# Gate weights folded between the row scales and the first evacuations, in an fp32-split encoder block

## The chip, the cores and the metric

One of the eight cores of a Trainium2 chip runs the kernel. The metric is device microseconds of one execution, the median over several runs. PE is TensorE (matmuls), DVE is VectorE, ACT is ScalarE, POOL is GpSimd, SP is the engine that issues most DMAs. Each takes its instructions strictly in the order in which they stand in its own queue and waits on semaphores for the others.

## The reference

One encoder layer on x of 512 positions by 1024 channels, float32. Only the first part matters here: RMS norm, one big input projection, a depthwise conv with SiLU on the 2048 mLSTM channels, block-diagonal q, k, v, and input and forget gates that are linear in q, k, v.

```python
h = rmsnorm(x, norm_w[l])                       # x * rsqrt(mean(x*x) + 1e-6) * norm_w
proj = h @ w_in[l]
x_f, z_f, x_m, z_m, o_m, g_logits = jnp.split(proj, split_points, axis=-1)
...
x_c = jax.nn.silu(centred_dwconv(x_m, conv_w[l], conv_b[l]))
q = block_diag_proj(x_c, w_q[l])                # blocks of 4 x 4
k = block_diag_proj(x_c, w_k[l])
v = block_diag_proj(x_m, w_v[l])
qkv = jnp.concatenate([q, k, v], axis=-1)
i_fwd = transpose(qkv @ w_igate_fwd[l] + b_igate_fwd[l])
f_fwd = log_sigmoid(transpose(qkv @ w_fgate_fwd[l] + b_fgate_fwd[l]))   # and both for bwd
...                                             # mLSTM in chunks both ways, Fourier branch, merge, norm
```

## The kernel before

Every large product is made of three matmuls. A float32 operand is split into a high part that TensorE's fp32r format holds (`hi_of`, an ACT copy) and the rest (`lo_of`, a DVE subtraction), and `mm3` adds high*high, high*low and low*high (lines 97 to 99). x is split once, scaled by norm_w, into the tiles hhi and hlo. Everything is laid out with channels in partitions, so one *unit* is 128 output channels of a projection: a weight tile of 128x1024 (8 blocks of 128 input channels), 24 matmuls of 128x512 into one PSUM bank `acc`. The raw weights of a unit come by DMA into a ring of three `raw` tiles (`fetch`, on SP), are split into `whi` and `wlo` (`prepare`), of which there are two buffers each, and are used by `proj`. `unit` prepares one unit ahead, so a unit's high half can be written only when PE has finished the unit two before it.

The row scales of the RMS norm are not applied to x but to the products. ACT squares the eight x tiles (L249), DVE adds them (L252), `norm_rows` sums over channels by matmuls with a column of ones (L311), DVE makes mean plus epsilon from that (rc, L312), POOL raises it to -0.5 (L313). `norm_bcast` puts the four scale columns on diagonals (L318, ACT), multiplies them with ones on PE (L320) and copies the result to SBUF as `rb` (L321, ACT): the 512 scales in every partition. `evac` multiplies a finished bank with rb (L366, DVE).

Units run in this order. Units 0 to 2 (one z unit and the first two conv units) are interleaved while x arrives (`first_units`). Units 3 to 16 are the other conv units, two more z units follow. Unit 3 carries the broadcast as a hook: `RB_AT = (3, 2)` puts it before its third block. From unit 3 on each bank is evacuated, from unit 4 on (`CONV_AT`) each evacuated tile goes through `conv`: one ACT operation, four DVE multiply-adds (L333), a Silu on ACT (L335).

The gate weights are folded with the blocks of q, k, v, so that the gates are products of the conv output and of its input. `load_gates` loads six tiles of 128x512 into the places of x tiles (vhi0, vlo0, vhi1, vlo1, vhi2, vlo2), which are free after the splits and the squares; `fold_gates(n)` multiplies one by the block weights and sums over four (two DVE operations, L282 and L283). In the kernel before the loads are issued with unit 5 and one fold goes with each of units 8 to 13; the last of them also fills `w_gate` (tiles wf0, wf1; L287 DVE, L288 ACT). `gate_mm` then makes the 32 gate matmuls (L301), after the second to last unit of this part; the first of them reads the output of the last conv.

What sets the order: a scheduler in the framework estimates durations and reorders instructions of each engine, except that those wrapped in `pin` keep their program order among one another. The code's order is therefore not always the queue's order.

Of the kernel before, what the change touches and what calls it, by code (L numbers as in the profile page):

```python
# [26 lines left out]
RB_AT = (3, 2)  # L27
LOAD_AT, FOLD_AT, CONV_AT, DRAIN_AT = 5, 8, 4, 12
# [12 lines left out]
def hybrid_block(ctx: ExitStack, tc, xT, xn, first, units, blocks, vecs, gates, gbias, consts, dft, fnw, out):  # L41
# [100 lines left out]
    def prepare():  # L142
        i = state["split"]
        r = raw_unit(i)
        extra = i >= first_pair and i % 4 >= 2
        hi = tl("gwh" if extra else "whi", [P, 1024], F32R, bufs=2)
        lo = tl("gwl" if extra else "wlo", [P, 1024], F32R, bufs=2)
        w = 1024 if len(plan[i]) == 2 else plan[i][0].shape[1]
        hi_of(hi[:, 0:w], r[:, 0:w])
        lo_of(lo[:, 0:w], r[:, 0:w], hi[:, 0:w])  # L150
        items.append((hi, lo))
        state["split"] += 1
        fetch()
# [91 lines left out]
    for g in range(2):  # L245
        part = []
        for k in range(4):
            sq = tl(f"{('sa', 'sb')[g]}{k}", [P, S])
            pin(se.activation(sq, xt[4 * g + k], AF.Square))  # L249
            part.append(sq)  # L250
        for k in range(1, 4):
            ve.tensor_tensor(out=part[0], in0=part[0], in1=part[k], op=ALU.add)  # L252
        sqs.append(part[0])

# [9 lines left out]
    grep, folded = {}, []  # L264
# [10 lines left out]
    def fold_gates(n):  # L275
        if n == 0:
            folds.extend([tl("vhi3", [P, 2, 16, 16]), tl("vlo3", [P, 1, 16, 16])])
        j, half = n // 2, n % 2
        hs = slice(8 * half, 8 * half + 8)
        g = grep[j, half]  # L280
        w = wview((V_WQ, V_WK, V_WV)[j])[:, hs].unsqueeze(2).to_broadcast([P, 8, 16, 4])
        pin(ve.tensor_tensor(out=g, in0=g, in1=w, op=ALU.mult))  # L282
        ve.tensor_reduce(out=folds[j // 2][:, j % 2, hs, :], in_=g, axis=AX.X, op=ALU.add)  # L283
        if n == 5:
            folded.append(True)
            f = folds[0]
            ve.tensor_tensor(out=w_gate[0][:, :, 0:16], in0=f[:, 0], in1=f[:, 1], op=ALU.add)  # L287
            se.activation(w_gate[1][:, :, 0:16], folds[1][:, 0], AF.Copy)  # L288
# [18 lines left out]
    def norm_rows():  # L307
        ssq = bank("wk", cols=4)
        for b in range(4):
            for g in range(2):  # L310
                pin(te.matmul(ssq[:, b : b + 1], sqs[g][:, b * P : (b + 1) * P], ones[:, 0:1], start=g == 0, stop=g == 1))  # L311
        ve.tensor_scalar(out=rc, in0=ssq, scalar1=1.0 / D, scalar2=EPS, op0=ALU.mult, op1=ALU.add)  # L312
        gp.tensor_tensor(out=rc, in0=rc, in1=mhalf[:, 0:1].to_broadcast([P, 4]), op=ALU.pow)  # L313

    def norm_bcast():
        diag = tl("sa15", [P, 4, P])
        for b in range(4):
            se.activation(diag[:, b], ident, AF.Copy, scale=rc[:, b : b + 1])  # L318
        rbp = bank("wk")
        pin(te.matmul(rbp, ones, diag.rearrange("p b c -> p (b c)"), start=True, stop=True))  # L320
        se.activation(rb, rbp, AF.Copy)  # L321
# [21 lines left out]
    def first_units():  # L343
        accs = [bank(t) for t in ("acc", "wk", "acc")]
        for n in range(4):
            for i, ((wh, wl), acc) in enumerate(zip(firsts, accs)):
                last = n == 3 and i == 2
                if last:
                    norm_rows()
# [5 lines left out]
    def proj(hooks={}):  # L355
        wh, wl = unit()
        acc = bank("acc")
        for k in range(8):
# [3 lines left out]
            mm3(acc, wh[:, ks], wl[:, ks], hv(x_hi, k), hv(x_lo, k), k == 0, k == 7, any(at <= k for at in hooks))  # L362
        return acc

    def evac(dst, acc, func=None):
        ve.tensor_tensor(out=dst, in0=acc, in1=rb, op=ALU.mult)  # L366
# [16 lines left out]
    for n, (kind, i) in enumerate([("z", 0)] + [("x", i) for i in XO]):  # L383
# [3 lines left out]
        acc = early[n] if n < NU0 else proj(hooks)  # L387
# [6 lines left out]
        if n >= RB_AT[0]:  # L394
            for j, *args in waiting:
                evac(*args)
# [3 lines left out]
        if n == LOAD_AT:  # L400
            load_gates()
        if n >= CONV_AT and ready:
            conv(ready.pop(0))
        while n >= DRAIN_AT and ready:
            conv(ready.pop(0))
        if FOLD_AT <= n < FOLD_AT + 6:
            fold_gates(n - FOLD_AT)
# [741 lines left out]
```

## Time and profile before

| | |
|---|---|
| median of three runs | 766.57 us (764.42 to 767.64) |
| the profiled execution | 765.64 us, its span 763.5 us |
| mean granted TensorE clock | 0.995 |
| PE busy | 751.3 us, 98% of the span |
| DVE, ACT, POOL busy | 526.3, 412.6, 69.0 us |
| DMA | 128.55 MB, mean 168 GB/s |

The span runs from the first to the last instruction of the core; the time of the execution is about 2 us longer. In rows of the profile the first number is a start in us from the beginning of the span, the second a duration; `[0.52 <-ACT whi L90]` means that the engine sat idle 0.52 us before and that ACT's write of whi at line 90 ended it. In a table of stretches each engine has its busy time and, in brackets, the number of its instructions; PEclk is the granted clock. L-numbers are lines of the kernel before. Matmuls overlap, so a stretch with PE busy throughout is judged by how far apart the matmuls start.

### The profile page before, as it was taken

Reading aid. Unit: us, or ns where it says so; the run is one execution under the profiler, and the core shown is the slowest. Engines: PE = TensorE matmul, PEld = TensorE weight load, DVE = VectorE, ACT = ScalarE, POOL = GpSimd, SP = SyncE. Lnnn points to the kernel's source line nnn. Section 1 sums busy time; section 2 is a strip of 40 time slices with the busy share of each in tenths; the row PEclk is TensorE's granted clock in tenths of the full one; section 3 lists DMA queues with packets and bytes.
Section 4 is the critical chain, followed back from the end, with each engine's and each line's share of the span. In section 5 each row is a group of like instructions: output and inputs, shape, how many; then the busy total and the mean of one; then the engine's idle time right before and its main releaser. Section 6 shows DMA issues by size and latency. Waiting matters only on the chain.

```text
span 763.5 us, 10954 instructions
## 1 busy us (share of the span) xinstructions
PE 751.3 (98%) x4146; PEld 645.2 (85%) x4146; DVE 526.3 (69%) x820; ACT 412.6 (54%) x649; POOL 69.0 (9%) x147
## 2 busy tenths in 40 slices
PE   9999999999999999999999999999999999999996
PEld 8778884888888888888888888899999999988885
DVE  7499993687758565866585757257667687556876
ACT  7444456559456842785264343266544577543444
POOL 0000000013200400041002110000020100000003
PEclk9999999999999999999999999999999999999998
DMA  8157766175852883378404973367655446554452
GB/s 299 55 206 234 225 191 197 50 216 154 175 174 85 253 203 122 120 211 224 135 28 150 224 236 117 101 197 210 193 165 152 135 153 197 176 180 144 145 193 110
DMA packets 40805, 128.55 MB, mean 168 GB/s; under 512 B 4785, under 2 KB 5426, under 8 KB 35634
## 3 DMA queue, kind: packets, MB, share of 16 engines
q1 hardware_dynamic: 36658, 104.14, 40.5%
q0 software_dynamic: 3520, 23.07, 15.0%
q8 instruction: 32, 0.52, 0.3%
q10 hardware_dynamic: 576, 0.66, 0.2%
q14 instruction: 19, 0.16, 0.1%
HBM read 125.76 MB, written 44.04 MB: 222 GB/s over the span
## 4 chain that ended last, share of the span: by engine, by line
PE 95%; DVE 2%; ACT 1%; issue 1%; POOL 0%; POOLq 0%; ACTq 0%
PE acc L97 17%; PE acc L99 17%; PE acc L98 17%; PE wk L97 7%; PE wk L99 7%; PE wk L98 7%; PE acc L556 3%; PE acc L557 3%; PE acc L558 3%; PE wk L627 2%; PE acc L999 1%; PE acc L998 1%; PE acc L997 1%; PE wk L301 1%; PE wk L659 1%; PE wk L196 1%
## 5 line engine op out<-in xcount | busy, mean ns | idle before, releaser
L93 DVE TENSOR_TENSOR wlo<-raw,whi 128x1024 fp32r<-128x1024 f32 (+2 forms) x107 | 125.1, 1172 | 79.5 <-ACT whi L90 78.3
L90 ACT ACTIVATE whi<-raw 128x1024 fp32r<-128x1024 f32 (+2 forms) x107 | 108.6, 1019 | 121.8 <-PE acc L98 71.1
L97 PE MATMUL acc<-hhi,whi 128*128 128x512 f32 x240 | 95.2, 397 | 0.7 <-ACT whi L90 0.7
L99 PE MATMUL acc<-hhi,wlo 128*128 128x512 f32 x240 | 94.0, 393 | 1.2 <-DVE wlo L93 1.2
L98 PE MATMUL acc<-hlo,whi 128*128 128x512 f32 x240 | 94.0, 392 | 0.0
L93 DVE TENSOR_TENSOR gwl<-raw,gwh 128x1024 fp32r<-128x1024 f32 (+1 forms) x39 | 47.2, 1209 | 18.0 <-ACT gwh L90 17.9
L90 ACT ACTIVATE gwh<-raw 128x1024 fp32r<-128x1024 f32 (+1 forms) x39 | 40.9, 1049 | 31.6 <-PE acc L98 11.2
L97 PEld LDWEIGHTS acc<-hhi,whi 128*128 128x128 f32 x240 | 45.5, 190 | 11.7 <-ACT whi L90 1.6
L99 PEld LDWEIGHTS acc<-hhi,wlo 128*128 128x128 f32 x240 | 45.4, 189 | 11.3 <-DVE wlo L93 1.7
L98 PEld LDWEIGHTS acc<-hlo,whi 128*128 128x128 f32 x240 | 45.4, 189 | 9.5 <-issue 0.2
L558 PE MATMUL acc<-whi,hlo 128*128 128x512 f32 x128 | 50.4, 394 | 0.0
L557 PE MATMUL acc<-wlo,hhi 128*128 128x512 f32 x128 | 50.4, 393 | 0.0
L98 PE MATMUL acc<-sb,whi 128*128 128x512 f32 x128 | 50.1, 391 | 0.0
L97 PE MATMUL acc<-sa,whi 128*128 128x512 f32 x128 | 49.8, 389 | 0.0
L98 PE MATMUL wk<-vlo,phi 128*128 128x512 f32 x128 | 49.8, 389 | 0.0
L97 PE MATMUL wk<-vhi,phi 128*128 128x512 f32 x128 | 49.6, 389 | 0.0
L99 PE MATMUL acc<-sa,wlo 128*128 128x512 f32 x128 | 49.0, 391 | 0.0
L99 PE MATMUL wk<-vhi,plo 128*128 128x512 f32 x128 | 48.0, 389 | 0.0
L556 PE MATMUL acc<-whi,hhi 128*128 128x512 f32 x128 | 47.7, 393 | 0.0
L333 DVE SCALAR_TENSOR_TENSOR t2k<-sa,vecs,t2k 128x511 f32<-128x511 f32 (+1 forms) x64 | 45.4, 744 | 0.3 <-ACT t2k L330 0.3
L93 DVE TENSOR_TENSOR vlo<-wk,vhi 128x512 fp32r<-128x512 f32 x32 | 20.6, 677 | 16.3 <-ACT vhi L90 16.3
L98 PEld LDWEIGHTS wk<-vlo,phi 128*128 128x128 f32 x128 | 24.0, 188 | 5.0
(411 smaller groups left out, 1916.8 us busy)
## 6 DMA issues: line engine op xcount, KB each, us to landing
raw<-in_units_dram SPq DMA_DIRECT2D x69, 512.0 KB, 4.1
sum<-in_blocks_dram SPq DMA_DIRECT2D x20, 1024.0 KB, 8.3
raw<-sum SPq DMA_DIRECT2D x64, 256.0 KB, 3.6
raw<-in_blocks_dram SPq DMA_DIRECT2D x48, 256.0 KB, 3.9
sum<-in_blocks_dram POOLq DMA_DIRECT2D x10, 1024.0 KB, 9.8
sum<-sum POOLq DMA_DIRECT2D x10, 1024.0 KB, 8.8
raw<-sum SPq DMA_DIRECT2D x8, 512.0 KB, 4.4
raw<-in_blocks_dram SPq DMA_DIRECT2D x6, 512.0 KB, 4.2
```

The costliest lines, as they stand in the source:

```text
L90: pin(se.activation(dst, src, AF.Copy, scale=scale), pinned)
L93: pin(ve.tensor_tensor(out=dst, in0=src, in1=hi.bitcast(F32), op=ALU.subtract), pinned)
L97: pin(te.matmul(acc, wh, xh, start=start, stop=False, **skip), pinned)
L98: te.matmul(acc, wh, xl, start=False, stop=False, **skip)
L99: te.matmul(acc, wl, xh, start=False, stop=stop, **skip)
L196: te.matmul(junk[:, 0:P], ones, ones, start=True, stop=True)
L301: pin(te.matmul(gate_ps[rows, :], w_gate[j][:, i, :], r, start=n == 0, stop=n == 14, tile_position=(0, 32 * (2 * b + j))), n + b + j > 0)
L333: ve.scalar_tensor_tensor(out=cv[:, o], in0=src[:, s], scalar=cw[k], in1=cv[:, o], op0=ALU.mult, op1=ALU.add)
L556: te.matmul(ops[t], hv(x_hi, k)[:, ts], wh[:, ks], start=k == 0, stop=False)
L557: te.matmul(ops[t], hv(x_hi, k)[:, ts], wl[:, ks], start=False, stop=False)
L558: te.matmul(ops[t], hv(x_lo, k)[:, ts], wh[:, ks], start=False, stop=k == 7)
L627: te.matmul(vp[:, ds], xm[c0 + d][:, b * P : (b + 1) * P], vbf[:, d, :], start=True, stop=True)
```

## The change

Nothing of the arithmetic's meaning changes; one addition replaces another. Its parts:

- The two sums of squares are added on DVE, so that `norm_rows` needs four matmuls instead of eight.
- `load_gates` is called in `first_units`, before the row sums, and the six folds stand right behind the row scales (before unit 3's matmuls in the program). `fill_gates` is a function of its own, called at unit 12.
- Units 3 and 4 are prepared before the row sums; the splits of the units up to 5 counted from the first prepared (i <= NU0 + 2) are pinned, and so are rc, the diagonals, rb, the folds, the evacuations of the banks that have waited, and the matmuls of unit 4.
- The broadcast stands before the fifth block of unit 3 (`RB_AT = (3, 4)`), and the first evacuations come with unit 4 instead of unit 3.

```diff
-RB_AT = (3, 2)
-LOAD_AT, FOLD_AT, CONV_AT, DRAIN_AT = 5, 8, 4, 12
+RB_AT = (3, 4)
+CONV_AT, DRAIN_AT = 4, 12
...
-        hi_of(hi[:, 0:w], r[:, 0:w])
-        lo_of(lo[:, 0:w], r[:, 0:w], hi[:, 0:w])
+        hi_of(hi[:, 0:w], r[:, 0:w], pinned=i <= NU0 + 2)
+        lo_of(lo[:, 0:w], r[:, 0:w], hi[:, 0:w], pinned=i <= NU0 + 2)
...
+    ve.tensor_tensor(out=sqs[0], in0=sqs[0], in1=sqs[1], op=ALU.add)
...
-        ve.tensor_reduce(out=folds[j // 2][:, j % 2, hs, :], in_=g, axis=AX.X, op=ALU.add)
-        if n == 5:
-            folded.append(True)
-            f = folds[0]
-            ve.tensor_tensor(out=w_gate[0][:, :, 0:16], in0=f[:, 0], in1=f[:, 1], op=ALU.add)
-            se.activation(w_gate[1][:, :, 0:16], folds[1][:, 0], AF.Copy)
+        pin(ve.tensor_reduce(out=folds[j // 2][:, j % 2, hs, :], in_=g, axis=AX.X, op=ALU.add))
+
+    def fill_gates():
+        f = folds[0]
+        ve.tensor_tensor(out=w_gate[0][:, :, 0:16], in0=f[:, 0], in1=f[:, 1], op=ALU.add)
+        pin(se.activation(w_gate[1][:, :, 0:16], folds[1][:, 0], AF.Copy))
...
-            for g in range(2):
-                pin(te.matmul(ssq[:, b : b + 1], sqs[g][:, b * P : (b + 1) * P], ones[:, 0:1], start=g == 0, stop=g == 1))
-        ve.tensor_scalar(out=rc, in0=ssq, scalar1=1.0 / D, scalar2=EPS, op0=ALU.mult, op1=ALU.add)
+            pin(te.matmul(ssq[:, b : b + 1], sqs[0][:, b * P : (b + 1) * P], ones[:, 0:1], start=True, stop=True))
+        pin(ve.tensor_scalar(out=rc, in0=ssq, scalar1=1.0 / D, scalar2=EPS, op0=ALU.mult, op1=ALU.add))
...
                 if last:
+                    load_gates()
+                    prepare()
+                    prepare()
                     norm_rows()
...
+        if n == NU0:
+            for m in range(6):
+                fold_gates(m)
-        acc = early[n] if n < NU0 else proj(hooks)
+        acc = early[n] if n < NU0 else proj(hooks, n == NU0 + 1)
...
-        if n >= RB_AT[0]:
+        if n > RB_AT[0]:
             for j, *args in waiting:
-                evac(*args)
+                evac(*args, pinned=len(waiting) > 1 and j != i)
...
-        if n == LOAD_AT:
-            load_gates()
...
+        if n == DRAIN_AT:
+            fill_gates()
...
-        if FOLD_AT <= n < FOLD_AT + 6:
-            fold_gates(n - FOLD_AT)
```

How the queues move at three places. In their rows stand line, operation, the tile written, `<-` and the tiles read, and a size; numbers tell buffers and writes of a name apart. The lines of the changed kernel lie one to four lines higher (L283 for L282, L369 for L366).

DVE before, from rc to the low half of unit 5 (wlo_70); sz0, sa4, sa5 are the evacuations of units 0 to 2, sa6 and sa7 of 3 and 4, t2k tiles are convs:

```order
L312 TENSOR_SCALAR rc_50_240<-wk_54_310 128x4
L366 TENSOR_TENSOR sz0_55_327<-acc_51_241,rb_49_239 128x512
L366 TENSOR_TENSOR sa4_57_329<-wk_52_242,rb_49_239 128x512
L366 TENSOR_TENSOR sa5_58_330<-acc_53_243,rb_49_239 128x512
L333 SCALAR_TENSOR_TENSOR t2k_74_415<-sa4_57_329,vecs_11_108,t2k_74_415 128x510
L333 SCALAR_TENSOR_TENSOR t2k_87_468<-sa5_58_330,vecs_11_108,t2k_87_468 128x510
L333 SCALAR_TENSOR_TENSOR t2k_74_415<-sa4_57_329,vecs_11_108,t2k_74_415 128x511
L366 TENSOR_TENSOR sa6_68_376<-acc_65_343,rb_49_239 128x512
L366 TENSOR_TENSOR sa7_73_413<-acc_72_388,rb_49_239 128x512
L333 SCALAR_TENSOR_TENSOR t2k_87_468<-sa5_58_330,vecs_11_108,t2k_87_468 128x511
L93 TENSOR_TENSOR wlo_70_383<-raw_61_335,whi_69_382 128x1024
```

DVE in the change, the same place; four pairs of L283 and L284 on vhi0, vlo0, vhi1 and vlo1 stand between rc and the first row here, and wlo_78 is unit 5's low half:

```order
L283 TENSOR_TENSOR vhi2_58_319<-vhi2_58_319,vecs_11_108 128x512
L288 TENSOR_TENSOR wf0_44_230<-vhi3_71_352 128x16x16
L284 TENSOR_REDUCE vlo3_72_353<-vhi2_58_319 128x128
L283 TENSOR_TENSOR vlo2_59_321<-vlo2_59_321,vecs_11_108 128x512
L284 TENSOR_REDUCE vlo3_72_353<-vlo2_59_321 128x128
L93 TENSOR_TENSOR wlo_78_401<-raw_62_327,whi_77_400 128x1024
L369 TENSOR_TENSOR sz0_67_348<-acc_51_242,rb_49_240 128x512
L369 TENSOR_TENSOR sa4_69_350<-wk_52_243,rb_49_240 128x512
L369 TENSOR_TENSOR sa5_70_351<-acc_53_244,rb_49_240 128x512
L369 TENSOR_TENSOR sa6_76_399<-acc_73_366,rb_49_240 128x512
L369 TENSOR_TENSOR sa7_81_431<-acc_80_406,rb_49_240 128x512
L333 SCALAR_TENSOR_TENSOR t2k_82_438<-sa4_69_350,vecs_11_108,t2k_82_438 128x510
```

The folds and the fill of wf0 now lie between rc and unit 5's low half, and that low half lies ahead of all evacuations instead of behind five of them and four conv steps.

PE before, from the end of unit 3 (acc_65) to unit 5 (acc_79) and unit 6 (acc_92); unit 4 is acc_72:

```order
L97 MATMUL acc_65_343<-hhi3_18_133,whi_59_331 128x512
L98 MATMUL acc_65_343<-hlo3_22_137,whi_59_331 128x512
L99 MATMUL acc_65_343<-hhi3_18_133,wlo_60_332 128x512
L98 MATMUL acc_72_388<-hlo3_22_137,whi_62_337 128x512
L99 MATMUL acc_72_388<-hhi3_18_133,wlo_63_338 128x512
L97 MATMUL acc_79_429<-hhi0_15_130,whi_69_382 128x512
L98 MATMUL acc_79_429<-hlo0_19_134,whi_69_382 128x512
L97 MATMUL acc_92_482<-hhi0_15_130,whi_76_423 128x512
L98 MATMUL acc_92_482<-hlo0_19_134,whi_76_423 128x512
L99 MATMUL acc_79_429<-hhi0_15_130,wlo_70_383 128x512
```

PE in the change at the same place; unit 4 is acc_80, unit 5 acc_87:

```order
L98 MATMUL acc_80_406<-hlo3_22_137,whi_63_329 128x512
L99 MATMUL acc_80_406<-hhi3_18_133,wlo_64_330 128x512
L97 MATMUL acc_87_452<-hhi0_15_130,whi_77_400 128x512
L98 MATMUL acc_87_452<-hlo0_19_134,whi_77_400 128x512
L99 MATMUL acc_87_452<-hhi0_15_130,wlo_78_401 128x512
```

Before, most of unit 4 was drawn ahead of unit 3, which therefore ended last, and units 5 and 6 began together. Now units 3, 4, 5 and 6 follow one another, and L320 stands after the first twelve matmuls of unit 3 instead of near the end of unit 4.

ACT before, around the split for the unit after the gate matmuls (whi_224) and the Silu of the last conv (sb3):

```order
L90 ACTIVATE phi2_171_939<-sb2_170_937 128x512
L90 ACTIVATE whi_224_1230<-raw_184_992 128x1024
L335 ACTIVATE sb3_179_982<-t2k_178_976 128x512
L368 ACTIVATE sz1_56_328<-sz1_56_328 128x512
L468 ACTIVATE half_r_195_1094<-half_194_1090 128x256
```

ACT in the change, the same place:

```order
L371 ACTIVATE sz0_67_348<-sz0_67_348 128x512
L335 ACTIVATE sb3_179_979<-t2k_178_973 128x512
L90 ACTIVATE phi3_180_981<-sb3_179_979 128x512
L90 ACTIVATE whi_224_1227<-raw_184_989 128x1024
L658 ACTIVATE sb3_179_979<-sb3_179_979,vecs_11_108 128x512
```

The Silu of the last conv has moved ahead of the split. On SP the six gate loads stand directly behind unit 4's raw load, ahead of unit 5's; before they stood behind unit 8's. From the gate matmuls on, all queues read as before apart from buffer numbers.

More of the change, by code (lines that the diff above doesn't have):

```diff
@@ L262, in hybrid_block @@
     ve.tensor_scalar(out=m4, in0=m4, scalar1=float(512.0 ** -0.5), scalar2=None, op0=ALU.mult)
-    grep, folded = {}, []
+    grep = {}
     def load_gates():
@@ L317, in norm_bcast @@
         for b in range(4):
-            se.activation(diag[:, b], ident, AF.Copy, scale=rc[:, b : b + 1])
+            pin(se.activation(diag[:, b], ident, AF.Copy, scale=rc[:, b : b + 1]))
         rbp = bank("wk")
         pin(te.matmul(rbp, ones, diag.rearrange("p b c -> p (b c)"), start=True, stop=True))
-        se.activation(rb, rbp, AF.Copy)
+        pin(se.activation(rb, rbp, AF.Copy))
     kept = []
@@ L353, in first_units, with proj @@
         return accs
-    def proj(hooks={}):
+    def proj(hooks={}, pinned=False):
         wh, wl = unit()
@@ L361, in proj, with evac @@
             ks = slice(k * P, (k + 1) * P)
-            mm3(acc, wh[:, ks], wl[:, ks], hv(x_hi, k), hv(x_lo, k), k == 0, k == 7, any(at <= k for at in hooks))
+            mm3(acc, wh[:, ks], wl[:, ks], hv(x_hi, k), hv(x_lo, k), k == 0, k == 7, pinned or any(at <= k for at in hooks))
         return acc
-    def evac(dst, acc, func=None):
-        ve.tensor_tensor(out=dst, in0=acc, in1=rb, op=ALU.mult)
+    def evac(dst, acc, func=None, pinned=False):
+        pin(ve.tensor_tensor(out=dst, in0=acc, in1=rb, op=ALU.mult), pinned)
         if func:
```

## The prediction

> **What bounds the kernel now.** I read the page first: span, busy shares, granted clock, chain.
>
> ```profile
> span 763.5 us, 10954 instructions
> PE 751.3 (98%) x4146; PEld 645.2 (85%) x4146; DVE 526.3 (69%) x820; ACT 412.6 (54%) x649; POOL 69.0 (9%) x147
> ...
> PEclk9999999999999999999999999999999999999998
> ...
> PE 95%; DVE 2%; ACT 1%; issue 1%; POOL 0%; POOLq 0%; ACTq 0%
> ```
>
> PE is the kernel: 98% busy and 95% of the chain. So an edit is worth only what it takes out of PE's own queue or out of a gap in it. All edits lie in the first 120 us, so next I asked for the stretches there.
>
> ```profile
> core 0: us, PE busy (x) PEld busy (x) DVE busy (x) ACT busy (x) POOL busy (x), PEclk, DMA share, GB/s
> 21.03:22.73 1.70, 1.70 (x18) 1.70 (x16) 1.54 (x2) 1.07 (x2) 0.00 (x0) 1.00 0.00 0
> 23.62:32.27 8.65, 8.65 (x38) 6.79 (x37) 0.00 (x0) 1.88 (x5) 1.02 (x1) 1.00 0.34 115
> 35.79:42.76 6.97, 5.01 (x13) 3.07 (x12) 6.97 (x11) 2.51 (x3) 0.00 (x0) 0.76 0.31 95
> 42.76:116.25 73.49, 73.49 (x326) 60.83 (x324) 71.26 (x101) 35.62 (x47) 2.71 (x3) 1.00 0.72 223
> 116.25:118.12 1.87, 0.38 (x2) 0.03 (x1) 1.42 (x3) 1.68 (x3) 0.00 (x0) 1.00 0.99 368
> ```
>
> From top to bottom: the row sums hold PE for 1.70 us. While the row scales travel to VectorE and back (8.65 us), DVE does nothing at all. Then PE works 5.01 of 6.97 us, at a mean clock of 0.76. Then it runs 73.49 us without a hole: 324 weight loads, 0.227 us for each matmul, 24 of them (5.45 us) a unit; DVE is busy 71.26 of these 73.49 us. Last there is a hole before the gate matmuls. PE's own rows for the first hole:
>
> ```profile
> 35.79 0.39 PE L99 MATMUL acc<-hhi,wlo 128*128 128x512 f32 x1
> 36.70 0.50 PE L97 MATMUL acc<-hhi,whi 128*128 128x512 f32 x1 [0.52 <-ACT whi L90]
> ...
> 37.65 0.50 PE L97 MATMUL acc<-hhi,whi 128*128 128x512 f32 x1 [0.21 <-ACT whi L90]
> ...
> 39.61 0.79 PE L99 MATMUL acc<-hhi,wlo 128*128 128x512 f32 x1 [1.23 <-DVE wlo L93]
> 40.20 0.63 PE L97 MATMUL acc<-hhi,whi 128*128 128x512 f32 x1
> ...
> 42.33 0.59 PE L99 MATMUL acc<-hhi,wlo 128*128 128x512 f32 x1
> 42.76 0.39 PE L97 MATMUL acc<-hhi,whi 128*128 128x512 f32 x1
> ```
>
> Unit 5 is not ready: its high half comes late from ACT, its low half (wlo) later still from DVE, and when PE starts again its matmuls are 0.43 us apart until 42.76. Why the halves are late stands in the rows of the engines that make them:
>
> ```profile
> 31.64 0.60 ACT L321 ACTIVATE rb<-wk 128x512 f32<-128x512 f32 x1 [5.59 <-PE wk L320]
> 35.59 2.01 ACT L90 ACTIVATE whi<-raw 128x1024 fp32r<-128x1024 f32 x2 [0.47 <-ACT t2k L330]
> ...
> 32.27 0.69 DVE L366 TENSOR_TENSOR sz<-acc,rb 128x512 f32<-128x512 f32 x1 [8.65 <-ACT rb L321]
> 36.48 1.28 DVE L366 TENSOR_TENSOR sa<-acc,rb 128x512 f32<-128x512 f32 x2
> 37.68 0.74 DVE L333 SCALAR_TENSOR_TENSOR t2k<-sa,vecs,t2k 128x511 f32<-128x511 f32 x1
> 38.34 1.22 DVE L93 TENSOR_TENSOR wlo<-raw,whi 128x1024 fp32r<-128x1024 f32 x1
> ```
>
> The high half begins at 35.59, because in the old order PE finishes unit 3, whose buffer it takes, last. The low half would have been possible about a microsecond later but stands on DVE behind two evacuations and a conv step, until 38.34; these are so late because rb comes only at 31.64.
>
> **The change, part by part.**
>
> *Row sums.* Eight matmuls become four, for one more add on DVE. The eight hold PE 1.70 us, so four give back 0.85 (with a fixed part in the 1.70, 0.7 to 0.9). The add costs PE nothing if it ends before PE comes at 21.03:
>
> ```profile
> 18.53 1.49 DVE L252 TENSOR_TENSOR sb<-sb,sb 128x512 f32<-128x512 f32 x2
> ...
> 23.46 0.15 DVE L312 TENSOR_SCALAR rc<-wk 128x4 f32<-128x4 f32 x1
> 24.76 1.28 ACT L318 ACTIVATE sa<-consts,rc 128x128 f32<-128x128 f32 x4 [2.66 <-POOL rc L313]
> ...
> 24.21 0.40 PE L97 MATMUL acc<-hhi,whi 128*128 128x512 f32 x1
> 30.58 1.02 PE L320 MATMUL wk<-sa,ones 128*128 128x512 f32 x2
> ```
>
> The old adds end at 20.02; a further 0.7 makes 20.7, 0.3 before 21.03. What follows on DVE, the splits of units 3 and 4, waits for PE's buffers anyway and then rc stands at 23.46 as now.
>
> *The broadcast (L320) in place.* It leaves PE's queue at the same price, but twelve matmuls after unit 3 starts instead of in the middle of unit 4. Unit 3 starts at 24.21 now, so at 23.36 then; twelve matmuls later is 26.08. The diagonal it reads is written by 24.76 + 1.28 = 26.04. This is a tie: between 0 and 0.3 us of new wait; I take 0.1, for the signal. Then rb exists at about 27.8 (1.02 on PE, 0.60 on ACT) instead of 32.2.
>
> *Gates loaded and folded early.* Six loads go past the raw loads of units 5 to 8 on SP, and twelve DVE operations and an add move from the convs to the place behind rc:
>
> ```profile
> L282 DVE TENSOR_TENSOR vhi<-vhi,vecs 128x512 f32<-128x512 f32 x3 | 2.1, 686 | 0.0
> L283 DVE TENSOR_REDUCE vhi<-vhi 128x128 f32<-128x512 f32 x2 | 1.4, 678 | 0.0
> L287 DVE TENSOR_TENSOR wf<-vhi 128x256 f32<-128x256 f32 x1 | 0.4, 417 | 0.0
> L333 DVE SCALAR_TENSOR_TENSOR t2k<-sa,vecs,t2k 128x511 f32<-128x511 f32 x28 | 20.8, 744 | 0.0
> ...
> 42.33 0.43 SPq L271 DMA_DIRECT2D vlo<-in_gates_dram  x1
> ...
> 16.18 2.18 ACT L249 ACTIVATE sb<-vlo 128x512 f32<-128x512 f32 x4
> ...
> vlo<-in_gates_dram SPq DMA_DIRECT2D x3, 256.0 KB, 5.1
> ```
>
> The chain is 6 × 0.686 + 6 × 0.678 + 0.417 = 8.6 us, so from 23.6 to 32.2, where DVE has been idle for 8.65 us. The loads overwrite x tiles, so they wait on SP for the squares, which end at 18.36. Even if all six went out after that, at half a microsecond each (0.43 now), the last would land at 21.4 + 5.1 = 26.5, and the chain wants it only at its eleventh operation, near 30. Behind them SP holds unit 5's raw load: out by 22, landed by 27 at the same 5.1, wanted at 29.8. No cost; if the cover fails, unit 5 slips one for one. What stands behind the chain on DVE is unit 5's low half (1.22 us, done at 33.4) and the evacuations.
>
> *Units 3, 4, 5 in a row on PE, splits of 4 to 6 fixed.* Unit 3 ends at 23.36 + 5.45 + 1.02 (L320) = 29.8; ACT then splits unit 5 until 31; unit 4 ends at 35.3, and unit 5's third matmul, the first to need the low half, comes at 35.7. Margin 2.3 us. Five evacuations (0.69 each) and one conv step then fill DVE to 37.6, unit 6's low half to 38.8, and PE wants that at 41.2. Per unit DVE has 0.69 + 1.22 + 4 × 0.744 = 4.9 us of work against 5.45 of PE; with a fold pair it was 6.2. So the hole goes. Its size: 35.79 to 42.76 is 6.97 us, in which 12 matmuls start (the window counts one more, begun before). 12 × 0.227 = 2.72, so 4.25 us are lost. Of these the half-rate stretch from 39.61 to 42.76 is 3.15 − 7 × 0.227 = 1.56. Ends: 0 (DVE as late as before) and 4.25; I take 4.25, since both halves have 2 us in hand.
>
> The Trainium skill ("TensorE: Matmul & The Clock Gate", Part 1) says that the clock falls to half after an idle window of about 3.4 us. The longest gap here is 1.23 us and the clock fell all the same, so the row does not bear the rule out. By the rule the half rate is not these gaps' doing, the 1.56 us would stay, and the sum would be 1.56 less; by the rows it goes with them.
>
> *The gate matmuls.* The hole before 118.12:
>
> ```profile
> 115.64 0.74 DVE L333 SCALAR_TENSOR_TENSOR t2k<-sa,vecs,t2k 128x510 f32<-128x510 f32 x1
> ...
> 116.44 1.06 ACT L90 ACTIVATE whi<-raw 128x1024 fp32r<-128x1024 f32 x1 [2.58 <-PE acc L98]
> 117.41 0.61 ACT L335 ACTIVATE sb<-t2k 128x512 f32<-128x512 f32 x1
> ...
> 116.25 0.39 PE L99 MATMUL acc<-hhi,wlo 128*128 128x512 f32 x1
> 118.12 0.59 PE L301 MATMUL wk<-sb,wf 128*32 128x512 f32 x1 [1.49 <-issue]
> ```
>
> The view puts the gap down to "issue", but the first gate matmul reads the last conv's Silu, which ends at 118.02. Its conv ends on DVE at 116.38, and ACT does a split first, which itself waited for PE. In the new order the Silu stands ahead of that split, and the conv needs only 1.06 + 1.22 + 0.74 + 0.61 = 3.6 us after the last unit starts, of its 5.45. So 1.87 − 0.23 = 1.64 us go; ends 0 and 1.64, and I take the whole because 1.8 us are in hand. From the gate matmuls on, each engine's queue reads as before.
>
> *Sum.* 0.85 + 4.25 + 1.64 − 0.1 = 6.6 us out of PE's queue. Against the profiled execution: 765.64 − 6.6 = 759.0 (span 756.9). That execution lies 0.9 under the median of the three runs, 766.57; half of this added, 759.4.
>
> **The rivals.**
>
> *The gate hole stays.* If the gap is really PE's own issue, or the convs still end last on DVE, 1.64 come back: gain 5.0, 761.0. For it speaks the word "issue" and that DVE was busy 71.26 of 73.49 us; against it that the Silu ends 0.1 before the matmul starts.
>
> *The half rate stays.* A mechanism of this kernel apart from the gaps would keep seven matmuls at 0.43: gain 5.0 too, 761.0. Against it: 0.76 is the only stretch above under 1.00. The Trainium skill's rule told above ("TensorE: Matmul & The Clock Gate", Part 1) is the one that would have it so.
>
> *The hole only moves.* All convs now start after 36, four of them waiting, and on DVE evacuations and low halves stand between their steps. If two or three low halves (units 7 to 10) come late by more than their 2 us in hand, PE stands again for 3 to 4 us: gain 3, 763.0, no change that can be told. It begins to count when DVE runs 2 us behind the sketch above.
>
> *Slower: the fold chain holds unit 5.* The chain is fixed ahead of the low half of unit 5 and of all evacuations, in order. Each microsecond it ends after 34.5 (35.7 less 1.22) is one on PE, plus 1.56 when the clock falls. It costs more than the 6.6 it could bring only if it ends about 5 us past that, near 39.5, that is with its 13 operations at 1.2 us instead of 0.68, or with the first gate landing at 31; at 5 us more it is 771. No row is near.
>
> **How the numbers follow.** All three terms: 0.66, 759.4, its own range 757.5 to 761. One of the two 5.0 us cases: 0.18, 761.0 with runs up to 762.5. The hole moves: 0.12, 763.0. Slower: 0.04. Less than 0.5% (3.8 us) is about what a measurement here cannot tell from no change, so faster is 0.84, same 0.12, slower 0.04. The range reaches from 757.0 (the lowest run shown, 764.42, less the sum is 757.8, and somewhat for the ends of the terms) to 763.0.
>
> **What would show it.** Four row-sum matmuls and unit 3 starting at about 23.4. L320 at 26.1 to 26.4. DVE busy from 23.6 without waiting for a gate load, unit 5's low half done by 34. No PE gap over 0.3 us from 27 to the gate matmuls and a granted clock of 1.00 there. The first gate matmul near 111.5, at most 0.3 us after the last unit. After it all gaps as before, 6.6 us earlier. I am wrong if PE waits for wlo at unit 5 to 10, if L320 waits over 0.5 us for the diagonal, or if the gate matmuls still stand 1.5 us with the Silu long done.

## The result, and the profile after

The changed kernel takes 761.02 us (median of six runs, 760.12 to 761.49), the kernel before 766.37 in six runs beside them (764.42 to 767.64). The ratio is 0.9929, with a 95% interval of 0.9914 to 0.9943: 5.35 us or 0.7% faster, where 7.2 (766.57 to 759.4) had been forecast. The profiled execution took 761.03 us, its span 758.9. From its page:

```profile
span 758.9 us, 10938 instructions
...
PE 748.7 (99%) x4138; PEld 642.9 (85%) x4138; DVE 527.3 (69%) x821; ACT 412.5 (54%) x649; POOL 69.7 (9%) x147
...
PE 95%; DVE 1%; ACT 1%; DMA 1%; POOL 0%; issue 0%; ACTq 0%; POOLq 0%
```

PE is still the bound, now 99% busy. The chain has one new entry, DMA with 1%; it is the start, below. The stretches that answer to those shown of before, in the trace after (us, busy time of each engine with its instructions, granted clock, DMA share):

```profile
22.69:23.49 0.80, 0.80 (x9) 0.80 (x8) 0.65 (x1) 0.80 (x2) 0.00 (x0) 1.00 0.87 302
25.12:33.41 8.29, 8.04 (x34) 5.98 (x33) 8.12 (x16) 2.95 (x6) 1.41 (x1) 1.00 0.46 162
36.00:43.00 7.00, 7.00 (x33) 5.79 (x32) 6.44 (x10) 3.31 (x5) 0.00 (x0) 1.00 0.40 138
43.00:113.22 70.22, 70.22 (x311) 58.14 (x310) 65.77 (x91) 36.16 (x49) 2.71 (x3) 1.00 0.70 205
113.22:113.54 0.32, 0.32 (x2) 0.00 (x0) 0.27 (x1) 0.12 (x1) 0.00 (x0) 1.00 0.97 333
```

The row sums hold PE 0.80 us instead of 1.70. DVE works through the wait for the scales (8.12 of 8.29 us, where it had done nothing). The stall before units 5 and 6 is gone: 33 matmuls in 7 us at a clock of 1.00. The last matmul before the gates and the first gate matmul are 0.32 us apart, where they had been 1.87. Unit 5's low half starts at 33.32, and ACT's Silu of the last conv stands ahead of the split:

```profile
33.32 1.21 DVE L93 TENSOR_TENSOR wlo<-raw,whi 128x1024 fp32r<-128x1024 f32 x1
...
111.47 0.63 ACT L335 ACTIVATE sb<-t2k 128x512 f32<-128x512 f32 x1 [1.82 <-DVE t2k L333]
...
113.42 1.06 ACT L90 ACTIVATE whi<-raw 128x1024 fp32r<-128x1024 f32 x1 [0.66 <-PE acc L98]
```

Two things are not as drawn, though. The first stands at the very start, in code that the change does not touch. A split of the first weights on ACT, in the trace before and in the one after:

```profile
6.09 0.42 ACT L90 ACTIVATE whi<-raw 128x256 fp32r<-128x256 f32 x1 [0.83 <-DMA raw<-in_first_dram]
```

```profile
7.80 0.42 ACT L90 ACTIVATE whi<-raw 128x256 fp32r<-128x256 f32 x1 [2.47 <-DMA raw<-in_first_dram]
```

It waits for a 256 KB load, 2.47 us instead of 0.83. The row sums start at 22.69 instead of 21.03, and all that follows is 1.66 us late. The second is at the broadcast. POOL's power before, then the same row and PE's rows after:

```profile
23.70 1.02 POOL L313 TENSOR_TENSOR rc<-rc,mhalf 128x4 f32<-128x4 f32 x1 [21.52 <-DVE rc L312]
```

```profile
25.36 1.41 POOL L313 TENSOR_TENSOR rc<-rc,mhalf 128x4 f32<-128x4 f32 x1 [23.17 <-DVE rc L312]
```

```profile
27.49 0.39 PE L99 MATMUL acc<-hhi,wlo 128*128 128x512 f32 x1
28.13 1.12 PE L320 MATMUL wk<-sa,ones 128*128 128x512 f32 x2 [0.25 <-ACT sa L318]
28.70 0.80 PE L97 MATMUL acc<-hhi,whi 128*128 128x512 f32 x1
```

POOL took 1.02 us for this operation before and takes 1.41 now. L320 starts 0.64 us after the matmul ahead of it instead of 0.23. From there to the matmul behind L320 but one it costs PE 0.51 us more than before.

Since the start differs, the executions are compared below by the time from the first row sum (L311) to the first gate matmul (L301, in the kernel after L302): 118.12 − 21.03 = 97.09 before, 113.54 − 22.69 = 90.85 after, 6.24 us less. That is the change. From the gate matmuls on the two traces run alike, 4.6 us apart (6.24 less the 1.66 of the start).

### The profile page after: what moved, and what is told of

Read it like the earlier page. It is cut to its first block, busy times and chain, and to the rows that moved or that the text cites. A ratio compares the mean times of both kernels' runs of the same rounds, so it can differ in the third digit from the quotient of the medians.

```text
span 758.9 us, 10938 instructions
## 1 busy us (share of the span) xinstructions
PE 748.7 (99%) x4138; PEld 642.9 (85%) x4138; DVE 527.3 (69%) x821; ACT 412.5 (54%) x649; POOL 69.7 (9%) x147
## 4 chain that ended last, share of the span: by engine, by line
PE 95%; DVE 1%; ACT 1%; DMA 1%; POOL 0%; issue 0%; ACTq 0%; POOLq 0%
PE acc L97 17%; PE acc L99 17%; PE acc L98 17%; PE wk L97 8%; PE wk L99 8%; PE wk L98 8%; PE acc L561 3%; PE acc L562 3%; PE acc L560 3%; PE wk L631 2%; PE acc L1003 1%; PE acc L1002 1%; PE acc L1001 1%; PE wk L302 1%; PE wk L663 1%; DMA raw<-in_first_dram 1%
## 5 line engine op out<-in xcount | busy, mean ns | idle before, releaser
L333 DVE SCALAR_TENSOR_TENSOR t2k<-sa,vecs,t2k 128x510 f32<-128x510 f32 (+1 forms) x64 | 45.3, 745 | 0.2
```

The source lines that it names most:

```text
L333: ve.scalar_tensor_tensor(out=cv[:, o], in0=src[:, s], scalar=cw[k], in1=cv[:, o], op0=ALU.mult, op1=ALU.add)
```

## Experiments

The first theory was that the change does what was drawn, less 0.4 us at L320, and that the rest of the distance between 6.6 and 5.35 is the start, which differs from one execution to the next. The rival was that the change itself delays the start. A second question was which part of the change clears which hole. What came of all of them:

| kernel | median us (runs) | profiled execution: L311 to first gate matmul | wait of the split for the 256 KB load | POOL, L313 |
|---|---|---|---|---|
| before | 766.37 (6) | 97.09 | 0.83 | 1.02 |
| before, again | 766.37 (1) | 95.65 | 3.15 | 1.03 |
| after | 761.02 (6) | 90.85 | 2.47 | 1.41 |
| after, again | 759.98 (5) | 90.85 | 2.87 | 1.41 |
| broadcast at block 6 | 760.61 (6) | 90.35 | 0.68 | 1.40 |
| folds behind the power | 760.63 (5) | 90.48 | 2.64 | 1.03 |
| eight row sums | 761.00 (5) | 91.24 | 1.02 | 1.40 |
| free order | 762.45 (5) | 92.22 | 2.58 | 1.40 |
| early folds alone | 763.56 (12) | 95.62 | 2.51 | 1.41 |
| all but the early folds | 767.99 (12) | 95.70 | 0.97 | 1.03 |
| first piece on SP | 759.41 (4) | 90.17 | none | 1.41 |
| the same, broadcast at block 6 | 759.45 (4) | 89.90 | none | 1.41 |
| before, first piece on SP | 765.13 (11) | 97.01 | none | 1.03 |

The kernel before had 765.82 to 766.20 in the comparisons beside these.

### The two kernels once more

No edit in either.

> The changed kernel once more, nothing edited. The first profile lost 1.66 us ahead of the row sums, where the code is the same: ACT's first high half waited 2.47 us for the first raw piece, 0.83 us in the kernel before. Theory A (a transfer that lands earlier or later from one execution to the next): the wait of that split differs again, between about 0.8 and 2.5 us, the row sums start between 21.0 and 22.7, and the whole execution's end moves by as much. Rival B (the change itself delays the start): the wait is about 2.5 us again and the row sums start at 22.6 or later. On both theories the broadcast (L320) waits about 0.4 us for the diagonal, since the reciprocal square root on POOL takes about 1.4 us beside the folds; time 760 to 761.5.

> The kernel before once more, nothing edited, for a second profile. Theory A (the start-up falls early or late from one execution to the next, and the half-rate stretch at units 5 and 6 comes and goes, both apart from the change): the mean clock is either 0.995, with matmuls 0.43 us apart somewhere between 39 and 44, or 0.998 without them and the stall some 1.5 us shorter; the first high half's wait is either about 0.8 or about 2.5 us. Rival B (both belong to the kernel): 0.83 us and 1.56 us as in the first profile.

After, again: 759.98 us, ratio 0.9930 (0.9916 to 0.9944). The split waited 2.87 us in its profile, and the row sums began at 22.96. Before, again: the split waited 3.15, longer than in any other profile:

```profile
8.36 0.42 ACT L90 ACTIVATE whi<-raw 128x256 fp32r<-128x256 f32 x1 [3.15 <-DMA raw<-in_first_dram]
```

So the late start is not the change's: of the ten profiles with this load on ACT's queue six show a wait of 2.47 us or more, the kernel before among them, and four one of 1.02 or less, three edits of the changed kernel among them. The 1.66 us by which the first profile after came short of the one before were the draw.

The second profile before has the same three gaps at units 5 and 6 as the first, to a few hundredths, and behind them something else. PE's rows, and a row of the table of stretches:

```profile
38.90 0.50 PE L97 MATMUL acc<-hhi,whi 128*128 128x512 f32 x1 [0.52 <-ACT whi L90]
...
39.85 0.50 PE L97 MATMUL acc<-hhi,whi 128*128 128x512 f32 x1 [0.21 <-ACT whi L90]
...
41.81 0.50 PE L99 MATMUL acc<-hhi,wlo 128*128 128x512 f32 x1 [1.24 <-DVE wlo L93]
42.15 0.40 PE L97 MATMUL acc<-hhi,whi 128*128 128x512 f32 x1
42.39 0.40 PE L98 MATMUL acc<-hlo,whi 128*128 128x512 f32 x1
```

```profile
38.00:43.00 5.00, 3.03 (x11) 1.60 (x10) 5.00 (x8) 2.50 (x3) 0.00 (x0) 1.00 0.08 12
```

After gaps of 0.52, 0.21 and 1.24 us the matmuls go on 0.23 to 0.34 us apart, and the clock is 1.00; in the first profile they stood 0.43 apart after the same gaps, at 0.76. The stretch to the gate matmuls is 1.44 us shorter for it. So the half-rate stretch follows the gaps only in some executions. The mean clocks suggest how many: in the 47 runs of the kernel before that stand beside these experiments it was 0.996 or less in 23 and 0.997 or 0.998 in the others; it was never under 0.997 in the eleven of the kernel after. A mean clock does not say where it fell, but of the four profiles with the old order on PE the three at 0.995 or 0.996 (before, early folds alone, and before with its first piece on SP) have the stretch behind these gaps, and the one at 0.998 has not. The 23 runs take 0.9 us more than the 24 in the mean (766.5 against 765.6). The gain of 6.24 us holds against an execution with it; against one without it the gain is 4.80. The 5.35 of the medians lies between.

### Which part clears which hole

All but the early folds: the changed kernel with the gates' loads, folds and fill where they were.

```diff
-                    load_gates()
...
-        if n == NU0:
-            for m in range(6):
-                fold_gates(m)
...
+        if n == 5:
+            load_gates()
...
+        if 8 <= n < 14:
+            fold_gates(n - 8)
```

> The changed kernel with the gate loads, folds and fill back where they were (loads after unit 5, a fold pair in each of units 8 to 13); the splits' and the broadcast's fixed order and the four row sums stay. Theory A (the stall at units 5 and 6 came from the order on PE and the late rb, the gate hole from the fold pairs among the convs): no stall between 30 and 43, a hole of up to 1.6 us before the first gate matmul, 0.3 to 1.6 us slower than the changed kernel; and POOL's reciprocal square root takes about 1.0 us again, as no DVE work stands beside it, so L320 waits 0.1 us or less. Rival B (the early folds are what clears the stall, since DVE is behind otherwise): PE stalls 2 us or more before unit 5 or 6, and the kernel is 3 to 6 us slower than the changed one.

It took 767.99 us, 1.0027 (1.0012 to 1.0041) of the kernel before: slower than before, and 7 us slower than after. The stall at units 5 and 6 is gone here too (from the matmuls behind L320 to the gates no two start over 0.3 us apart), as theory A had it; but all of it is back at the gate matmuls. PE's rows there, and the stretches:

```profile
111.77 0.39 PE L99 MATMUL acc<-hhi,wlo 128*128 128x512 f32 x1
117.31 1.03 PE L302 MATMUL wk<-sb,wf 128*32 128x512 f32 x1 [5.15 <-issue]
```

```profile
111.77:117.31 5.54, 0.39 (x2) 0.03 (x1) 4.35 (x6) 3.62 (x7) 0.00 (x0) 0.86 0.82 303
117.31:122.40 5.09, 5.09 (x24) 1.32 (x28) 0.69 (x1) 3.23 (x5) 0.00 (x0) 0.50 0.58 227
```

The first gate matmul stands 95.70 us behind the row sums, 95.65 to 97.09 in the kernel before: the last matmul of the units comes 5 us earlier (111.77 − 21.61 = 90.16; 116.25 − 21.03 = 95.22 before), the last conv's output hardly at all. DVE makes it, and DVE's queue shows no room:

```profile
112.81 0.74 DVE L333 SCALAR_TENSOR_TENSOR t2k<-sa,vecs,t2k 128x511 f32<-128x511 f32 x1
113.47 1.22 DVE L93 TENSOR_TENSOR wlo<-raw,whi 128x1024 fp32r<-128x1024 f32 x1
114.60 0.68 DVE L93 TENSOR_TENSOR mlo<-t2k,mhi 128x512 fp32r<-128x512 f32 x1
115.20 0.68 DVE L93 TENSOR_TENSOR plo<-sb,phi 128x512 fp32r<-128x512 f32 x1
115.80 0.74 DVE L333 SCALAR_TENSOR_TENSOR t2k<-sa,vecs,t2k 128x510 f32<-128x510 f32 x1
```

The last conv step starts at 115.80, behind three splits, and then come the Silu and the gates. On top of the gap of 5.5 us the first gate matmuls run at a clock of 0.50; all 16 steps of them take 9.57 us, 7.01 in the kernel after. Neither theory had this. Rival B had the loss (3 to 6 us) in the wrong place; theory A had the place and bounded the hole by the 1.6 us that it had before, as if the time gained upstream could not run into it.

Early folds alone: the kernel before with the loads and folds of the gates moved, nothing else.

```diff
+                    load_gates()
...
+        if n == NU0:
+            for m in range(6):
+                fold_gates(m)
...
-        if n == LOAD_AT:
-            load_gates()
...
-        if FOLD_AT <= n < FOLD_AT + 6:
-            fold_gates(n - FOLD_AT)
```

> The kernel before with one part of the change alone: the gates are loaded and folded between the row scales and the first evacuations. Order on PE, splits, broadcast and the eight row sums are those of the kernel before. Theory A (early folds fill idle time of DVE and clear only the gate hole): the stall before units 5 and 6 stays, 3.5 to 5.5 us with its half-rate stretch, the gate hole shrinks to about 0.3 us, and the kernel is 1.0 to 2.0 us faster than before, 3.5 to 5 us slower than the changed one. Rival B (the early folds clear the stall too): over 4 us faster than before. Rival C (without the fixed order they hold up unit 5): the stall grows beyond 6 us and the kernel is not faster than before.

763.56 us, 0.9979 (0.9965 to 0.9992). The stall stays, with the same three gaps and the half rate after them; the gate hole is gone:

```profile
38.30 0.50 PE L97 MATMUL acc<-hhi,whi 128*128 128x512 f32 x1 [0.52 <-ACT whi L90]
...
39.25 0.50 PE L97 MATMUL acc<-hhi,whi 128*128 128x512 f32 x1 [0.21 <-ACT whi L90]
...
41.21 0.80 PE L99 MATMUL acc<-hhi,wlo 128*128 128x512 f32 x1 [1.23 <-DVE wlo L93]
41.80 0.63 PE L97 MATMUL acc<-hhi,whi 128*128 128x512 f32 x1
42.23 0.63 PE L98 MATMUL acc<-hlo,whi 128*128 128x512 f32 x1
...
117.93 0.39 PE L99 MATMUL acc<-hhi,wlo 128*128 128x512 f32 x1
118.25 0.62 PE L301 MATMUL wk<-sb,wf 128*32 128x512 f32 x1
```

That is theory A. Its gain is 1.6 us by the ratio and 1.5 in the profiles (95.62 against 97.09, both with the half rate), within the 1.0 to 2.0 expected. In the medians it is 2.4 against the 765.95 beside it; only three of its twelve runs have a mean clock of 0.996 or less, against about half of the kernel before's. Together the two runs say how the parts add up. Early folds alone bring 1.5 to 2.4, the rest alone costs 2.0, both bring 5 to 6. The rest takes the stall out of PE's way, a DVE without room gives it back at the gates, and the folds make that room.

Free order: the changed kernel without the pins on unit 4's matmuls, on the splits and on the waiting evacuations.

```diff
-        hi_of(hi[:, 0:w], r[:, 0:w], pinned=i <= NU0 + 2)
-        lo_of(lo[:, 0:w], r[:, 0:w], hi[:, 0:w], pinned=i <= NU0 + 2)
+        hi_of(hi[:, 0:w], r[:, 0:w])
+        lo_of(lo[:, 0:w], r[:, 0:w], hi[:, 0:w])
...
-        acc = early[n] if n < NU0 else proj(hooks, n == NU0 + 1)
+        acc = early[n] if n < NU0 else proj(hooks)
...
-                evac(*args, pinned=len(waiting) > 1 and j != i)
+                evac(*args)
```

> The changed kernel without the fixed order of unit 4's matmuls, of the splits of units 4 to 6 and of the four waiting evacuations; the early folds, the four row sums and the broadcast's own place in the program stay. In the order that the scheduler then makes, PE mixes units 3 and 4 again, the broadcast comes after 35 of their matmuls instead of 12, and unit 5's low half stands behind five evacuations. Theory A (the fixed order is what clears the stall, the folds what clears the gate hole): PE stalls 3 to 5 us before units 5 and 6, no hole at the gate matmuls, 3 to 5 us slower than the changed kernel, near the kernel with early folds alone (763.6) less 0.9 for the row sums. Rival B (the early folds and the earlier broadcast are enough): within 1 us of the changed kernel.

762.45 us, 0.9955 (0.9941 to 0.9968), about 1.4 slower than after: between the two theories. Of the three gaps of the kernel before the first is down to 0.08 us and the second is gone; the third, for the low half, stays:

```profile
36.63 0.39 PE L99 MATMUL acc<-hhi,wlo 128*128 128x512 f32 x1
36.94 0.50 PE L97 MATMUL acc<-hhi,whi 128*128 128x512 f32 x1
37.27 0.40 PE L98 MATMUL acc<-hlo,whi 128*128 128x512 f32 x1
39.06 0.50 PE L99 MATMUL acc<-hhi,wlo 128*128 128x512 f32 x1 [1.39 <-DVE wlo L93]
```

```profile
37.19 0.68 DVE L369 TENSOR_TENSOR sa<-acc,rb 128x512 f32<-128x512 f32 x1
37.79 1.22 DVE L93 TENSOR_TENSOR wlo<-raw,whi 128x1024 fp32r<-128x1024 f32 x1
38.93 2.06 DVE L333 SCALAR_TENSOR_TENSOR t2k<-sa,vecs,t2k 128x511 f32<-128x511 f32 x3
```

Unit 5's low half stands behind five evacuations again and starts at 37.79, at 33.32 in the kernel after. So this run shows the pins' own worth: 1.37 us, or 1.9 with the 0.5 at L320 that this order does not pay. Its granted clock is 1.00 behind the gap of 1.39 us, and 0.997 or 0.998 in the mean of each of its five runs. Which of the parts that it keeps took the other two gaps and the half rate away was not tried by itself.

### The broadcast's wait

Broadcast at block 6, six matmuls later:

```diff
-RB_AT = (3, 4)
+RB_AT = (3, 6)
```

> The changed kernel with the broadcast two blocks (six matmuls, 1.4 us) later in unit 3, at block 6 instead of block 4. Theory A (L320's wait for the diagonal costs PE about 0.5 us, and rb has slack because the folds keep DVE until 33.4): no gap before L320, 0.4 to 0.5 us faster than the changed kernel; rb is ready at about 30.6, still ahead of the first evacuation. Rival B (the wait is refunded elsewhere, by slack on the way to the gate matmuls): same time within 0.2 us.

The wait is gone, and the stretch to the gate matmuls is 90.35, 0.50 us under the kernel after, as theory A had it. In the medians (760.61, 0.9932, 0.9916 to 0.9947) half a microsecond does not show: the runs fall between 758.76 and 761.33 with the start.

Folds behind the power: one small copy on DVE that reads POOL's result, ahead of the folds.

```diff
         if n == NU0:
+            pin(ve.tensor_copy(tl("fss0", [P, 4]), rc))
             for m in range(6):
                 fold_gates(m)
```

> The changed kernel with one tiny VectorE copy that reads the finished row scales ahead of the folds, so that the folds start only when POOL's reciprocal square root is done. Theory A (that POOL operation takes 1.41 us in the profiles with folds beside it and 1.03 us in the one without, because a VectorE operation with two SBUF inputs runs beside it; the Trainium skill, 'SBUF — State Buffer', says that such a pair contends for a shared port): POOL takes 1.0 us again and L320 waits 0.1 us or less for the diagonal, 0.4 us less on PE than in the changed kernel; the fold chain ends 1.3 us later, at about 34.7 with the late start, and unit 5's low half at 35.9, ahead of 37.7 when PE wants it. Rival B (the POOL operation is slowed by something else that came with the change, such as the gate loads): it takes 1.4 us again and L320 waits as before.

POOL's row and PE's, in that kernel:

```profile
25.34 1.03 POOL L313 TENSOR_TENSOR rc<-rc,mhalf 128x4 f32<-128x4 f32 x1 [23.16 <-DVE rc L312]
```

```profile
27.73 1.12 PE L320 MATMUL wk<-sa,ones 128*128 128x512 f32 x2
```

The gate loads are all there, only the folds start after the power, and it takes 1.03 us again; L320 does not wait, and the stretch is 90.48, 0.37 under after. Theory A. Over all profiles the operation takes 1.40 or 1.41 us in the eight with folds beside it and 1.02 or 1.03 in the five without. The low half of unit 5, later by 1.3 us, held nothing up. Which of the DVE operations beside the power lengthens it was not tried.

Eight row sums, the changed kernel without the added L254:

```diff
-    ve.tensor_tensor(out=sqs[0], in0=sqs[0], in1=sqs[1], op=ALU.add)
...
-            pin(te.matmul(ssq[:, b : b + 1], sqs[0][:, b * P : (b + 1) * P], ones[:, 0:1], start=True, stop=True))
+            for g in range(2):
+                pin(te.matmul(ssq[:, b : b + 1], sqs[g][:, b * P : (b + 1) * P], ones[:, 0:1], start=g == 0, stop=g == 1))
```

> The changed kernel with eight row-sum matmuls again and without the extra add (L254). Theory A (each row-sum matmul is PE time on the path): the row sums hold PE for 1.70 us against 0.80 and the kernel is 0.9 us slower than the changed one. Rival B (the saved time only lengthens L320's wait for the diagonal): L320 waits 0.4 us in both, and the time differs by less than 0.3 us.

```profile
23.83 1.40 POOL L313 TENSOR_TENSOR rc<-rc,mhalf 128x4 f32<-128x4 f32 x1 [21.65 <-DVE rc L312]
```

```profile
26.86 0.39 PE L99 MATMUL acc<-hhi,wlo 128*128 128x512 f32 x1
27.08 1.02 PE L320 MATMUL wk<-sa,ones 128*128 128x512 f32 x2
```

Between the theories. The row sums cost 0.90 us more, but L320 no longer waits, and 0.39 is left (91.24 against 90.85); 761.00 us in the medians. POOL starts 2.67 us after the first row sum in both kernels (23.83 − 21.16, 25.36 − 22.69): the row scales stand behind the low halves of units 3 and 4 on DVE, which four matmuls less do not hurry. So at the place where the broadcast stands more than half of the row sums' 0.90 became a wait.

### The start

First piece on SP: the load for which the split waits goes out on SP's queue.

```diff
-    nc.scalar.dma_start(starts[0][:, 256:768], first[0][:, 256:768])
     nc.sync.dma_start(xt[0], xT[0])
+    nc.sync.dma_start(starts[0][:, 256:768], first[0][:, 256:768])
```

> The changed kernel with one DMA issue moved: the 256 KB piece of the first weights that ACT's split waited 0.7 to 1.0 us for in three profiles and 2.5 to 2.9 us in three others goes out on SP's queue, behind the first x tile, instead of on ACT's. Theory A (the two starts of the kernel are this piece's, which shares the engines with the other queue's loads as it happens to come): the split never waits over 1 us, the row sums start at 21.0 to 21.3, and the runs cluster at 759.0 to 759.8 without those at 761. Rival B (all the start-up loads together are late, whatever the queue): the row sums still start at 21 in some profiles and 22.7 in others, with runs from 759.5 to 761.3; or the x tile that is now later holds PE up instead, at 761 or above.

> Both edits that may beat the changed kernel: the first piece on SP's queue, and the broadcast at block 6. Theory A: 0.5 us under the kernel with the first piece on SP alone, so about 758.7, with no gap before L320. Rival B (the start stays as it falls): a spread from 758.8 to 761.3 as with the broadcast alone.

> The kernel before with the 256 KB first piece on SP's queue, the edit that took the late starts out of the changed kernel (759.41). Theory A (the late start is a matter of the two kernels alike): no late start here either, 765.0 to 766.0, so that the distance of the two kernels with this edit is 5.6 to 6.6 us, nearer to the 6.6 that was forecast than the 5.2 to 6.0 measured without it. Rival B (the kernel before rarely started late): the time stays at 766.0 to 766.2 or rises.

After with this: 759.41 us, four runs from 758.83 to 759.89, 0.9905 (0.9890 to 0.9920) of the kernel before. The wait is gone and the runs lie within 1.1 us, 2.0 in the eleven of the kernel after. The row sums start at 22.25, not at 21.0 as theory A had it. PE's rows ahead of them:

```profile
6.62 0.58 PE L97 MATMUL acc<-hhi,whi 128*128 128x512 f32 x1
...
21.80 0.39 PE L97 MATMUL acc<-hhi,whi 128*128 128x512 f32 x1
22.02 0.39 PE L98 MATMUL acc<-hlo,whi 128*128 128x512 f32 x1
22.25 0.95 PE L311 MATMUL wk<-ones,sa 128*128 128x1 f32 x8
```

The first of the units' matmuls starts at 6.62, at 5.94 in the first profile before. And 68 of them stand ahead of the row sums here and with the broadcast at block 6 besides, 66 in every other profile: the order has changed, and the first two of unit 3 have moved ahead. These two are 0.45 us, so 0.45 of the 0.68 us by which this kernel's stretch is under the kernel after is only a later starting point; the other 0.22 is a shorter step to L320 (0.42 instead of 0.64). With the broadcast at block 6 besides, 759.45 (0.9906, 0.9893 to 0.9920): the stretch is 0.27 shorter and the median the same. Both beat the first runs of the kernel after in the medians by about 1.6 us and its second by 0.6; the intervals overlap.

The kernel before with it: 765.13 us (11 runs), 0.9985 (0.9975 to 0.9996), and its runs fall into two groups. Four have a mean clock of 0.997 or 0.998 and take 763.21 to 764.88 us; seven have 0.995 or 0.996 and take 765.12 to 766.03. That fits the half rate, which the profiled one (766.03, 0.996) has. The two kernels with this edit are 5.7 us apart.

## Why the prediction was right, and where it was not

The time alone proves little. 761.02 us is the number that the prediction gave to its two rivals of 5.0 us, and it lies at the very end of the range for all three terms (757.5 to 761). The traces decide: in the profiled execution all three terms came. Why the medians differ by less is told below.

*Row sums, 0.85.* Measured 0.90 (0.80 us against 1.70). The add cost PE nothing. The part by itself is worth less, 0.39 in the kernel with eight row sums, since the rest turned into the next term's wait.

*The broadcast, −0.1 of 0 to 0.3.* This is the term that was mis-sized: 0.51 us. The tie was drawn correctly, with the diagonal as late after the row sums as before; with the power at its old 1.03 us only 0.1 is left of it, in the kernels with the folds late or behind the power. What the working lacked is that the folds, which it moved beside POOL's power, make the power 0.39 us longer. It asked of the folds only whom they precede on DVE, not who works beside them. The text had named a wait over 0.5 us at L320 as a sign of being wrong; it came to 0.41, and 0.1 more between the two matmuls of L320.

*The stall, 4.25.* All of it came out of the profiled execution (97.09 to 90.85, after the other terms), and unit 5's low half was done at 34.5 instead of 33.4, with a start 1.66 us later. But the 1.56 of the half rate are in it, and they are there in about half of the executions only. The prediction took the half rate of one profile for a property of the kernel and set its sum against a median. In the medians that is worth an estimated 0.5 to 0.7 (half of the 0.9 between the two groups of runs, or half of the 1.44 between the two profiles). With the 0.4 at L320 beyond its 0.1 this makes 0.9 to 1.1 of the 1.25 missing from 6.6 to 5.35; the rest is small beside the spread of the start and stays open. The other 0.5 or so of the 7.2 is not a term of the change: the median of 766.57 lay 0.9 us above the profiled execution, and the forecast added only half of this to its time.

*The gate hole, 1.64.* Measured 1.55 (a step of 0.32 instead of 1.87). That the word "issue" hid the wait for the Silu was right: the Silu now starts at 111.47, ahead of the split at 113.42. But the sum treated this hole and the stall as two terms that add, though its working per unit (4.9 us of DVE's work, 6.2 with a fold pair, against 5.45 of PE's) already said that the folds are what takes DVE's room. The kernel without the early folds shows that they are one budget: DVE had 71.26 us of work in 73.49, so an earlier start of the units alone goes to the gate hole, all of it. The sum came out because the folds, 8.6 us of DVE's work, were moved into idle time, more than the 4.25 and the 1.64 together.

*Fold chain, loads, unit 5.* The chain waited for no load, and no load behind it was late. It ended at 33.41, forecast for 32.2 with a start 1.66 us earlier.

*The rivals.* The half rate did not stay: no row after the change shows it, as it follows gaps, if not each time. The rule of the Trainium skill ("TensorE: Matmul & The Clock Gate", Part 1) by which it would have stayed asks for an idle window of about 3.4 us. Where a run had such a gap, 5.5 us ahead of the gate matmuls, the clock was 0.50 for the next 5.1 us, and there rule and run agree. At units 5 and 6 the same three short gaps lowered the clock in one execution and not in another, with no gap over 1.24 us; there the measurement decides against the rule as it was drawn on. The Trainium skill says in the same part that the window runs freely, so that it falls differently on the same work; no run here shows the window itself. "The hole only moves" was given 0.12 at 763.0 and did not happen; as a mechanism it was the strongest of all, though at the gate matmuls and not at units 7 to 10: the kernel without the early folds shows it, 7 us slower than after. The slower case was not near.

The place of the start in its spread was no step of the prediction. It moves either kernel by up to 2.3 us (row sums from 20.92 to 23.23 in the ten profiles with the load on ACT's queue). The runs of the kernel after fall into 759.5 to 760.1 and 760.7 to 761.5, which fits an early and a late start; both of its profiles are of the late group.

## What to carry to other kernels

Two holes of PE that wait for the same engine are one budget: before adding their sizes, ask whether that engine has the room by which both can go. Here clearing the first alone lengthened the second to 5.5 us, with half the clock behind it. When work is moved into idle time, look at who works beside it there as well as at who stands behind it. And what one profile shows after a gap, or at the start, may be a draw: two profiles of the same kernel, or its runs' mean clocks, say whether it belongs to the kernel.

## What the runs showed of the hardware

A POOL operation on 128x4 elements takes 1.02 or 1.03 us alone and 1.40 or 1.41 with a DVE multiply of two SBUF operands beside it, and the DVE operation keeps its 0.68. The Trainium skill ("SBUF — State Buffer", Who interferes with whom) has a rule for this: a VectorE instruction with two SBUF inputs contends with a GpSimd instruction that reads SBUF, for a port pair that the section calls an exclusive lock, and the order of issue decides who is blocked. The direction agrees; in the trace after the power begins 0.51 us before the multiply's end (25.19 + 0.68) and is 0.38 longer, on an engine whose spans are rough. No run here shows the port itself.

PE's gaps of 0.52, 0.21 and 1.23 us were followed by some seven matmuls 0.43 us apart in the first profile of the kernel before and in the one with early folds alone. The same gaps were followed by none in the second profile of the kernel before.

A 256 KB load issued on ACT's queue at 1.7 us, among loads on SP's, kept its reader waiting 0.68 to 1.02 us in four profiles and 2.47 to 3.15 in six, with no code changed ahead of it.
